# First down projection of a hybrid decoder layer: chunk stores in four pieces on ScalarE's queue in place of one on GpSimd's

## The chip, the core and the metric

The kernel runs on one core of a Trainium2 chip. The time is the device time of one execution in microseconds (us), and a kernel's time is the median over its runs. Five engines work from queues of their own, each in order: TensorE (PE; its weight loads are PEld), VectorE (DVE), ScalarE (ACT), GpSimd (POOL) and SyncE (SP). A DMA is issued by an instruction on one of these queues (here SP, ACT or POOL) and lands later.

## The reference, cut to what matters

One layer, 1024 prompt tokens and 8 x 4 sample tokens, 1024 channels, 2816 hidden units:

```python
x = x + 0.5 * swiglu(rms_norm(x, g_ffn1), w1_ffn1, w3_ffn1, w2_ffn1)   # first FFN
p = rms_norm(x, g_mix) @ w_in        # q, k, v, forget gates, conv inputs
x = x + merge_groups(attention(q, k, v, logf, caches), bg, short_conv(uc), ...)
x = x + 0.5 * swiglu(rms_norm(x, g_ffn2), w1_ffn2, w3_ffn2, w2_ffn2)   # second FFN
```

with `swiglu(x, w1, w3, w2) = (silu(x @ w1) * (x @ w3)) @ w2`. The sample tokens attend to 2048 past positions in pages; `cache_logf` holds a forget value for each past row and head, and is read through the page table. Everything is float32; the kernel makes each product from three matmuls of rounded operands (L104 to L106: high x high, high x low, low x high).

## The kernel before, in words

The 1056 tokens are four chunks of 264, kept with channels on the partitions. The residual `x` of a chunk is 128 x 8 x 264.

**First up projection** (`up`, `blocked`, L277 to L340, and `plain` before it, up to about 92 us). For each block f of 128 hidden units it makes weight sums on DVE, splits them into high and low parts (ACT casts `wh`, L87; DVE subtracts `wl`, L89), and runs products of twelve matmuls each into one of eight PSUM banks (`bank`). DVE takes the products out of the banks and forms `t` = silu(gate) x up, at L326 and L330/L331. POOL stores every `t` to DRAM (`h_d`, L269, L327 and L332). `t` has two buffers: the next-but-one `t` can't be written before the store of the first has landed. Four stores belong to one f for both pairs of chunks, and two to the extra `blocked` call for one pair (f is then called e in `up`).

**First down projection** (`down`, L342). Its work is a list of sections, `DOWN1`: chunk 0 whole, chunks 1 and 2 up to hidden block 12, chunks 1 and 2 from block 12 on, chunk 3 whole. In each, eight output tiles d are computed for each chunk; DVE adds tile d to the residual (L408), ACT squares it (L124) and DVE sums the squares (L125). A tile is final when the chunk's last section has added it. When the chunk's sum of squares is known (`final`, then `done1`, L589), four things follow: the whole chunk is stored to `x_d` by POOL (L590; 1056 KB; the mix stage reads it back later), `rs` is computed (L170/L171), DVE scales all eight tiles **in place** (L190), and the scaled tiles are split into XH and XL (L193/L194), the operands of the mix. The scaling overwrites what the store reads, so it waits until the store has landed.

**past_gates** (L577) fetches the past forget values: 16 times two gathers of 64 KB each into the tile `R` (L468, POOL; `R` has one buffer), and one 128 KB store of `R` to `bs_d` (L587, POOL). It is called in `done1` of chunk 0 inside `tc.issue_after(stored)`.

**What sets the order.** A scheduler puts the instructions of each engine in order when the program is built; source order alone doesn't. `issue_after(ins)` binds what is issued inside it to stand behind `ins`, for the instructions on the engine of `ins`.

```python
t = small("t")                                      # blocked, L329 to L332
nc.vector.tensor_add(t, ps, z["u2"])
nc.vector.tensor_mul(t, t, z["s0"])
nc.gpsimd.dma_start(h_d[2 * p][:, f, :], t)
```

Of the kernel before, what the change touches and what calls it, by code (L numbers as in the profile page):

```python
# [46 lines left out]
DOWN1 = [((0,), 0, NF), ((1, 2), 0, 12), ((1, 2), 12, NF), ((3,), 0, NF)]  # L47
# [15 lines left out]
class Step:  # L63
# [275 lines left out]
            if f % 2 and 0 <= e < n0:  # L339
                self.blocked(w1, w3, e, (1,), ops, h_d)  # L340

    def down(self, w2, h_d, hp, x_of, done, sections, hb, ends=False):  # L342


        nc = self.nc
        xs, accs, sums, sqs, late = {}, {}, {}, {}, []

        def final(c):
            if c in sums:
                nc.tensor.matmul(sums[c], self.ones, sqs[c], start=False, stop=True)  # L350
            else:
                sums[c] = self.bank()
                self.stat(accs[c], sums[c])
            done(c, xs[c], sums[c])

        used, n0 = 0, min(hb, 14)
        before = {}
        for n, (cs, f0, f1) in enumerate(sections):
            end = n == len(sections) - 1
            hs, ins, loads = {}, {}, {}  # L360

            def weights(d):
                ws = []
                for g in range(f0, f1, 8):
                    m = min(8, f1 - g) * P
                    ws += self.weight(w2[d, :, g * P:g * P + m], m)
                loads[d] = self.last
                return ws

            spare = hb - live if n else 0  # L370
            ws = weights(0)
            j = 0
            for c in cs:
                hs[c] = []
                for f in range(f0, f1, 2):
                    u = used % hb
                    p, b = (hp[0], n0) if u < n0 else (hp[1], hb - n0)
                    h = p.tile([P, 2, 2, CH], F32R, tag="h", bufs=b, name="h")
                    used += 1
                    raw = h[:, 1].bitcast(F32)  # L380
                    tie = None
                    if n:
                        tie = before[1 + j * 6 // spare] if j < spare else loads[0]
                    with self.tc.issue_after(tie) if tie else nullcontext():
                        ins[c] = nc.sync.dma_start(raw, h_d[c][:, f:f + 2, :]).ins
                    j += 1
                    self.parts(h[:, 0], h[:, 1], raw)
                    hs[c] += [(h[:, 0, i, :], h[:, 1, i, :]) for i in range(2)]
            live = j
            for d in range(KD):  # L390
                if d:
                    self.after = ins[cs[0]] if d < 2 else None
                    ws = weights(d)
                    self.after = None
                if d == KD - 1:
                    before = loads
                for c in cs:
                    o = self.bank()
                    k = (f1 - f0) // 2
                    self.dot(o, ws[:k], hs[c][:k], stop=False)  # L400
                    if late and d % 4 == 0 and c == cs[-1]:
                        final(late.pop(0))
                    self.dot(o, ws[k:], hs[c][k:], start=False)
                    if d == 0 and f0 == 0:
                        with self.tc.issue_after(ins[c]) if n == 0 else nullcontext():
                            xs[c] = x_of(c)
                    x = xs[c][:, d, :]
                    nc.vector.scalar_tensor_tensor(x, o, 0.5, x, ALU.mult, ALU.add)  # L408
                    if f1 < NF:
                        continue  # L410
                    if ends and end:
                        if d == 0:
                            sums[c] = self.bank()
                        else:
                            nc.tensor.matmul(sums[c], self.ones, sqs[c], start=d == 1, stop=False)
                        sqs[c] = self.small("sq", 4)
                        nc.scalar.activation(sqs[c], x, AF.Square)
                    else:
                        if d == 0:
                            accs[c] = self.tmp.tile([P, CH], F32, tag="acc", bufs=2, name="acc")  # L420
                        self.sq_add(accs[c], d == 0, x)
                    if d == KD - 1:
                        late.append(c)
        for c in late:
            final(c)
# [3 lines left out]
def kernel(ctx: ExitStack, tc: tile.TileContext, io: dict):  # L429
    nc = tc.nc  # L430
    K = Step(tc, io)
# [6 lines left out]
    def pool(es, name, side="right", **kw):  # L438
        return es.enter_context(tc.tile_pool(name=name, bufs=1, side=side, reuse_waits="tile", **kw))
# [17 lines left out]
    def gain(col, k):  # L457
        return prm[:, col + k:col + k + 1]
# [8 lines left out]
    def gather(dst, src, ix):  # L467
        nc.gpsimd.indirect_dma_start(out=dst, out_offset=None, in_=src,  # L468
                                     in_offset=bass.IndirectOffsetOnAxis(ap=ix, axis=0))


    x_d = [dp.tile([P, KD, CH], F32, name=f"x_d{c}") for c in range(NCH)]
    x2_d = [dp.tile([P, KD, CH], F32, name=f"x2_d{c}") for c in range(NCH)]
    h1_d = [dp.tile([P, NF, CH], F32, name=f"h1_d{c}") for c in range(NCH)]
# [94 lines left out]
    with ExitStack() as es:  # L569
        hp = [pool(es, "h1", "left"), pool(es, "h1b", "left")]  # L570
        xp = pool(es, "x2")
        K.tmp = pool(es, "t2")

        def x_in(c):
            x = xp.tile([P, KD, CH], F32, tag="x", bufs=2, name="x")
            nc.sync.dma_start(x, io["xT"][c])
            return x  # L577

        def past_gates():

            for g in range(2):
                for i in range(8):
                    R = K.tmp.tile([P, 2, P], F32, tag="R", bufs=1, name="R")
                    for s in range(2):
                        col = PAGES - 1 - (2 * i + s)
                        gather(R[:, s, :], io["lf"], idl[:, g, col:col + 1])
                    nc.gpsimd.dma_start(bs_d[g][:, 256 * i:256 * i + 256], R.rearrange("p s k -> p (s k)"))  # L587

        def done1(c, x, ps):  # L589
            stored = nc.gpsimd.dma_start(x_d[c], x).ins  # L590
            rs = K.rstd(ps, D)
            cs = slice(c * CH, (c + 1) * CH)
            for k0 in range(0, KD, 4):
                for d in range(k0, k0 + 4):
                    K.scale(x[:, d, :], x[:, d, :], gain(G_MIX, d), rs)
                K.parts(XH[:, k0:k0 + 4, cs], XL[:, k0:k0 + 4, cs], x[:, k0:k0 + 4, :])
            if c == 0:
                with tc.issue_after(stored):
                    past_gates()

        K.nrs = 1
        K.down(io["w2a"], h1_d, hp, x_in, done1, DOWN1, 16, False)
    es_ps.close()

    es_w.close()
# [616 lines left out]
    with ExitStack() as es:  # L1222
        K.tmp = pool(es, "t3")
        xp = pool(es, "x3")
        xa, xs = [None] * NCH, [None] * NCH
# [66 lines left out]
    hp = [pool(ctx, "h2", "left"), pool(ctx, "h2b", "left")]  # L1292
# [118 lines left out]
```

## Time and profile before

| | us |
|---|---|
| median of 3 runs (lowest, highest) | 2117.48 (2117.12, 2118.97) |
| the profiled execution's own time | 2112.15 |
| its span, first to last instruction | 2110.1 |
| PE busy in the span | 2052.3 (97%) |
| DVE, ACT, POOL busy | 1344.5 (64%), 864.9 (41%), 336.2 (16%) |

The profile is of one execution. A timeline row gives the start and the length of an instruction, its engine and line, what it writes and reads, how many like it follow one another, and in brackets how long its engine had been idle and what ended that. Idle time of an engine counts only if the engine that bounds the kernel waits for it. The granted clock is TensorE's, as a share of 2.4 GHz.

### The profile page before, as it was taken

What the parts mean: (1) busy time and instruction counts of PE and PEld (TensorE: products, weight loads), DVE (VectorE), ACT (ScalarE), POOL (GpSimd) and SP (SyncE); (2) the same over time, 40 slices, a digit from 0 to 9 for tenths busy, and PEclk for the clock granted to TensorE, in tenths of its full rate; (3) what the DMA queues carried; (4) which work ended last, traced back from release to release, by engine and by line L of the source; (5) the groups of instructions that cost most, each with busy time, mean ns of one, the idle gap of its engine ahead of it and who ended that gap; (6) DMA issues with size and microseconds to landing.
All of it is one profiled execution on the core that took longest, in us unless ns stands there. A gap on an engine that the chain in (4) does not pass through costs nothing.

```text
span 2110.1 us, 44486 instructions
## 1 busy us (share of the span) xinstructions
PE 2052.3 (97%) x17570; PEld 1969.2 (93%) x17570; DVE 1344.5 (64%) x2586; ACT 864.9 (41%) x1734; POOL 336.2 (16%) x487
## 2 busy tenths in 40 slices
PE   7999999999999889999999989999999999999998
PEld 7999999999999878789997768999999999999997
DVE  8877777777645753222226777886777777775364
ACT  6533333345434432212116664553333343464243
POOL 0011111110233023343433410000101111100000
PEclk9999999999999999999999999999999999999999
DMA  6222222247655679997858525422222222586353
GB/s 217 79 92 93 90 86 87 86 140 267 230 165 171 212 233 349 358 349 236 286 164 194 138 60 177 138 95 81 82 72 83 82 92 87 169 305 200 109 182 126
DMA packets 139617, 341.02 MB, mean 162 GB/s; under 512 B 30000, under 2 KB 46592, under 8 KB 137872
## 3 DMA queue, kind: packets, MB, share of 16 engines
q1 hardware_dynamic: 82704, 218.15, 32.1%
q0 software_dynamic: 28736, 88.50, 12.5%
q10 hardware_dynamic: 27968, 31.54, 4.8%
q8 instruction: 138, 2.26, 0.5%
q14 instruction: 71, 0.58, 0.1%
HBM read 279.75 MB, written 58.33 MB: 160 GB/s over the span
## 4 chain that ended last, share of the span: by engine, by line
PE 55%; DVE 3%; ACT 1%; DMA 1%; issue 1%; POOL 0%; SPq 0%; ACTq 0%; DVEq 0%; POOLq 0%
PE ps L105 12%; PE ps L104 12%; PE ps L106 12%; PE pg L104 4%; PE pg L106 4%; PE pg L105 4%; PE pv L884 1%; PE sc L841 1%; PE O L1157 1%; PE ptp L1143 1%; DVE nm L1129 1%; PE S L1124 1%; PE ps L143 1%; DMA KA<-k_d 1%; DVE Pr L1134 0%
## 5 line engine op out<-in xcount | busy, mean ns | idle before, releaser
L105 PE MATMUL ps<-op,wh 128*128 128x264 f32 x2604 | 741.0, 285 | 1.1 <-DVE op L194 1.0
L106 PE MATMUL ps<-op,wl 128*128 128x264 f32 x2604 | 738.2, 284 | 0.0
L104 PE MATMUL ps<-op,wh 128*128 128x264 f32 x2604 | 737.4, 284 | 0.4 <-ACT s L265 0.4
L87 ACT CAST wh<-wraw 128x512 fp32r<-128x512 f32 x542 | 315.9, 600 | 464.8 <-PE ps L105 297.7
L105 PEld LDWEIGHTS ps<-op,wh 128*128 128x128 f32 x2604 | 489.1, 188 | 2.2 <-DVE op L194 1.9
L104 PEld LDWEIGHTS ps<-op,wh 128*128 128x128 f32 x2604 | 489.5, 188 | 1.2 <-ACT s L265 0.6
L106 PEld LDWEIGHTS ps<-op,wl 128*128 128x128 f32 x2604 | 490.2, 188 | 0.2
L89 DVE TENSOR_TENSOR wl<-wraw,wh 128x512 fp32r<-128x512 f32 x542 | 350.6, 662 | 204.0 <-ACT wh L87 189.9
L106 PE MATMUL ps<-h,wl 128*128 128x264 f32 x1408 | 398.9, 283 | 8.8 <-DVE wl L89 8.8
L104 PE MATMUL ps<-h,wh 128*128 128x264 f32 x1408 | 402.6, 286 | 0.0
L105 PE MATMUL ps<-h,wh 128*128 128x264 f32 x1408 | 401.1, 285 | 0.0
L106 PEld LDWEIGHTS ps<-h,wl 128*128 128x128 f32 x1408 | 265.7, 189 | 9.0 <-DVE wl L89 9.0
L104 PEld LDWEIGHTS ps<-h,wh 128*128 128x128 f32 x1408 | 265.5, 189 | 0.2
L105 PEld LDWEIGHTS ps<-h,wh 128*128 128x128 f32 x1408 | 265.5, 189 | 0.2
L104 PE MATMUL pg<-XH,wh 128*128 128x352 f32 x576 | 190.4, 331 | 0.9 <-DVE z L698 0.9
L106 PE MATMUL pg<-XH,wl 128*128 128x352 f32 x576 | 185.7, 322 | 1.3 <-DVE wl L89 1.1
L105 PE MATMUL pg<-XL,wh 128*128 128x352 f32 x576 | 185.4, 322 | 0.0
L87 ACT CAST wh<-s 128x512 fp32r<-128x512 f32 x176 | 107.8, 616 | 117.3 <-PE ps L105 108.2
L327 POOL DMA_DIRECT2D h_d<-t x79 | 42.8, 542 | 600.4 <-DVE t L326 596.3
L89 DVE TENSOR_TENSOR wl<-s,wh 128x512 fp32r<-128x512 f32 x176 | 120.4, 689 | 25.9 <-ACT wh L87 21.3
L104 PEld LDWEIGHTS pg<-XH,wh 128*128 128x128 f32 x576 | 108.6, 189 | 18.0 <-issue 16.8
L106 PEld LDWEIGHTS pg<-XH,wl 128*128 128x128 f32 x576 | 108.7, 189 | 1.8 <-DVE wl L89 1.8
(273 smaller groups left out, 2576.0 us busy)
## 6 DMA issues: line engine op xcount, KB each, us to landing
wraw<-in_w2a SPq DMA_DIRECT2D x48, 512.0 KB
wraw<-in_w2b SPq DMA_DIRECT2D x48, 512.0 KB
h_d<-t POOLq DMA_DIRECT2D x176, 132.0 KB, 2.0
h<-h_d SPq DMA_DIRECT2D x88, 264.0 KB
kvraw<-in_kc SPq DMA_DIRECT2D x64, 256.0 KB
kvraw<-in_vc SPq DMA_DIRECT2D x64, 256.0 KB
wraw<-in_w1a SPq DMA_DIRECT2D x28, 512.0 KB
wraw<-in_w3a SPq DMA_DIRECT2D x28, 512.0 KB
```

The source lines that it names most:

```text
L87: nc.scalar.copy(wh, x)
L89: nc.vector.tensor_sub(wl, x, wh)
L104: nc.tensor.matmul(ps, w[0], x[0], start=start, stop=False)
L105: nc.tensor.matmul(ps, w[0], x[1], start=False, stop=False)
L106: nc.tensor.matmul(ps, w[1], x[0], start=False, stop=stop)
L143: nc.tensor.matmul(ps, self.ones, sq, start=n == 0, stop=n == len(xs) - 1)
L327: nc.gpsimd.dma_start(h_d[2 * p + 1][:, f, :], t)
L841: nc.tensor.matmul(ps[quarter(hp)], QZ[:, g, hp, 32 * b4:32 * b4 + 32], raw[:, :, hp * P:hp * P + P], start=b4 == 0, stop=b4 == 3)
L884: nc.tensor.matmul(pv[quarter(hp), cs], PT[:, 4 * j + s, quarter(hp)], raw[:, s, hp * P:hp * P + P], start=j == 0 and s == 0, stop=False)
L1124: nc.tensor.matmul(S[:, k0:k1], QA[:, qs], KA[:, k0:k1], start=True, stop=False)
L1129: nc.vector.tensor_reduce(nm, S[:, :nk], AX.X, ALU.max, negate=True)
L1143: nc.tensor.transpose(pt_[:, j * P:(j + 1) * P], Pr[:, (j0 + j) * P:(j0 + j + 1) * P], ident)
```

## The change

`down` gets a function `part`, which it calls after every second output tile of a chunk's last section (d = 1, 3, 5, 7). The first down projection passes `store`, which stores two finished tiles (128 x 528, 264 KB) from ACT's queue. `done1` no longer stores. `past_gates` stays inside `issue_after`, which now names the last piece of chunk 0, an instruction on ACT.

```diff
-    def down(self, w2, h_d, hp, x_of, done, sections, hb, ends=False):
+    def down(self, w2, h_d, hp, x_of, done, sections, hb, ends=False, part=None):
...
                     if f1 < NF:
                         continue
+                    if part and d % 2:
+                        part(c, xs[c], d - 1)
...
+        stored = {}
+
+        def store(c, x, d):
+            stored[c] = nc.scalar.dma_start(x_d[c][:, d:d + 2, :], x[:, d:d + 2, :]).ins
+
         def done1(c, x, ps):
-            stored = nc.gpsimd.dma_start(x_d[c], x).ins
             rs = K.rstd(ps, D)
...
             if c == 0:
-                with tc.issue_after(stored):
+                with tc.issue_after(stored[0]):
                     past_gates()
...
-        K.down(io["w2a"], h1_d, hp, x_in, done1, DOWN1, 16, False)
+        K.down(io["w2a"], h1_d, hp, x_in, done1, DOWN1, 16, False, store)
```

In the changed file lines behind L410 lie two lower, and those behind L590 six lower: the gathers are L470, the store to `bs_d` is L589, the pieces are L594.

The order of instructions on PE is the same. On POOL it is not. This is POOL's order of the changed kernel against that of before in the first up projection, from the last store of `plain` (L269) over the stores of f = 6 (L327, L332) to the first of f = 7. `h1_d` is the DRAM copy of the hidden units; `R` and `bs_d` belong to `past_gates`.

```order
 L269 DMA h1_d1_84<-t_1115 128x264
+L470 DMA R_7390<-in_lf,idl_73 128x128 x2
+L589 DMA bs_d0_119<-R_7390 128x256
+L470 DMA R_7394<-in_lf,idl_73 128x128 x2
+L589 DMA bs_d0_119<-R_7394 128x256
+L470 DMA R_7398<-in_lf,idl_73 128x128 x2
 L327 DMA h1_d1_84<-t_1399 128x264
 L327 DMA h1_d3_86<-t_1417 128x264
+L589 DMA bs_d0_119<-R_7398 128x256
 L332 DMA h1_d0_83<-t_1433 128x264
+L470 DMA R_7402<-in_lf,idl_73 128x128 x2
 L332 DMA h1_d2_85<-t_1450 128x264
```

Gathers now stand ahead of and between the stores of `t`. The pattern goes on over f = 7, 8 and 9; this is its end, up to the stores of the extra call with e = 0.

```order
 L332 DMA h1_d2_85<-t_2248 128x264
+L589 DMA bs_d1_120<-R_7446 128x256
+L470 DMA R_7450<-in_lf,idl_73 128x128 x2
+L589 DMA bs_d1_120<-R_7450 128x256
 L327 DMA h1_d3_86<-t_2385 128x264
 L332 DMA h1_d2_85<-t_2401 128x264
```

All 32 gathers and 16 stores of `R` stand ahead of the store of `t_2385`. In the down projection the same 48 instructions are gone from POOL, and with them the whole-chunk stores; the last rows of that piece of the difference:

```order
-L468 DMA R_7447<-in_lf,idl_73 128x128 x2
-L587 DMA bs_d1_120<-R_7447 128x256
-L590 DMA x_d1_76<-x_7342 128x2112
-L590 DMA x_d2_77<-x_7469 128x2112
-L701 MEMSET zt_10018 128x72
-L590 DMA x_d3_78<-x_9006 128x2112
```

Before, the stores of chunks 1 and 2 stood behind the whole of `past_gates`. On ACT the last pieces of chunks 1 and 2 now stand in front of the squares of the same tiles (`sq`), several casts ahead of `rs` and XH of chunk 1 (ACT of the changed kernel):

```order
L594 DMA x_d1_76<-x_7346 128x528
L124 ACTIVATE sq_8814<-x_7346 128x264
...
L594 DMA x_d2_77<-x_7472 128x528
L124 ACTIVATE sq_8850<-x_7472 128x264
...
L170 ACTIVATE rs_8968<-ps_8961,eps_68 128x264
...
L193 CAST XH_6374<-x_7346 128x4x264
```

## Rows read from the trace of the kernel before

**Rows 1.** The page's busy time, share of span and instructions of each engine.

```profile
PE 2052.3 (97%) x17570; PEld 1969.2 (93%) x17570; DVE 1344.5 (64%) x2586; ACT 864.9 (41%) x1734; POOL 336.2 (16%) x487
```

**Rows 2.** PE's waits, 470 to 840 us: total us, times, longest.

```profile
PE ps L106 <- DVE wl L89: 8.8, 1, 8.8
PE ps L135 <- ACT ah L133: 2.3, 1, 2.3
...
PE pg L104 <- DVE z L698: 0.9, 1, 0.9
```

**Rows 3.** Timeline of PE around its longest wait: start, us, instruction, idle before.

```profile
683.51 0.28 PE L105 MATMUL ps<-h,wh 128*128 128x264 f32 x1
692.61 0.59 PE L106 MATMUL ps<-h,wl 128*128 128x264 f32 x1 [8.81 <-DVE wl L89]
...
697.38 0.28 PE L106 MATMUL ps<-h,wl 128*128 128x264 f32 x1
```

**Rows 4.** Timeline of DVE, 660 to 700 us.

```profile
674.80 1.80 DVE L171 RECIPROCAL rs<-rs 128x264 f32<-128x264 f32 x1
676.51 0.63 DVE L89 TENSOR_TENSOR wl<-wraw,wh 128x512 fp32r<-128x512 f32 x1
687.71 2.92 DVE L190 SCALAR_TENSOR_TENSOR x<-x,prm,rs 128x264 f32<-128x264 f32 x7 [10.57 <-DMA x_d<-x]
```

**Rows 5.** Timeline of POOL, 540 to 690 us.

```profile
543.98 1.02 POOL L468 DMA_INDIRECT R<-in_lf,idl  x1 [0.56 <-DMA wraw<-in_w2a]
...
590.06 0.97 POOL L468 DMA_INDIRECT R<-in_lf,idl  x1 [1.85 <-DMA bs_d<-R]
...
603.91 0.97 POOL L468 DMA_INDIRECT R<-in_lf,idl  x1 [1.94 <-DMA bs_d<-R]
...
652.05 0.96 POOL L468 DMA_INDIRECT R<-in_lf,idl  x1 [3.50 <-DMA bs_d<-R]
...
658.53 0.97 POOL L468 DMA_INDIRECT R<-in_lf,idl  x1 [1.86 <-DMA bs_d<-R]
...
678.27 0.97 POOL L468 DMA_INDIRECT R<-in_lf,idl  x1 [3.58 <-DMA bs_d<-R]
...
682.71 0.59 POOL L587 DMA_DIRECT2D bs_d<-R  x1 [2.22 <-DMA R<-in_lf,idl]
683.29 1.10 POOL L590 DMA_DIRECT2D x_d<-x  x2
```

**Rows 6.** Timeline of DVE at chunk 3's end.

```profile
745.55 1.67 DVE L764 COPY selh<-cst 8x128 f32<-8x128 f32 x1
...
753.92 2.92 DVE L190 SCALAR_TENSOR_TENSOR x<-x,prm,rs 128x264 f32<-128x264 f32 x7 [3.87 <-DMA x_d<-x]
```

**Rows 7.** The DMA issues: count, KB each, median us to landing.

```profile
h_d<-t POOLq DMA_DIRECT2D x176, 132.0 KB, 2.0
...
x_d<-x POOLq DMA_DIRECT2D x4, 1056.0 KB, 6.1
```

**Rows 8.** Windows: us, busy (count) of PE, PEld, DVE, ACT, POOL, clock, DMA share, GB/s.

```profile
92.00:183.00 91.00, 91.00 (x752) 91.00 (x751) 72.80 (x144) 35.33 (x73) 8.95 (x17) 1.00 0.27 86
544.00:683.00 139.00, 139.00 (x1149) 139.00 (x1149) 74.89 (x138) 55.37 (x103) 43.75 (x48) 1.00 0.56 183
683.00:698.00 15.00, 6.19 (x34) 5.98 (x33) 9.44 (x17) 4.11 (x6) 1.39 (x3) 0.66 0.65 235
...
590.00:604.00 14.00, 14.00 (x118) 14.00 (x117) 3.80 (x7) 1.71 (x4) 5.09 (x7) 1.00 0.20 55
```

**Rows 9.** Timeline of POOL, 85 to 185 us.

```profile
182.71 0.54 POOL L327 DMA_DIRECT2D h_d<-t  x1 [7.68 <-DVE t L326]
```

**Rows 10.** Timeline of DVE, 88 to 113 us.

```profile
90.52 1.25 DVE L230 TENSOR_TENSOR d<-x,d 128x1056 f32<-128x1056 f32 x1
...
112.69 0.43 DVE L330 TENSOR_TENSOR t<-ps,u 128x264 f32<-128x264 f32 x1 [0.58 <-DMA h_d<-t]
```

**Rows 11.** Line L468's gathers of `R`: duration ns min/median/max, first and last start.

```profile
L468 POOL DMA_INDIRECT R<-in_lf,idl x32: 941/972/1565, 544.0 to 679.5; - x32
```

## The prediction, as it stood before the changed kernel was run

> **What bounds the kernel now.** I read the page first, for which engine bounds the span: PE is busy in 97% of it [rows 1]. A change can only give back what PE waits, or make it wait anew, so the next view is PE's waits around the first down projection. Three are worth naming: 8.8 us for a `wl` of DVE, 2.3 us for `ah` of ACT, and 0.9 us for DVE's `z` [rows 2]. PE's timeline then shows the large one as a hole: the last matmul before it starts at 683.51, the next at 692.61 [rows 3].
>
> DVE's timeline says why that `wl` was late. DVE works in order. It made its last `wl` before the hole at 676.51 (0.63 long), then sat idle for 10.57 us, until 687.71, in front of the scaling of chunk 1, and what ended the idle time was the landing of an `x_d` store [rows 4]. POOL's timeline says why the store was late: `past_gates` fills POOL's queue from 543.98 until the last `bs_d` store at 682.71, and the two `x_d` stores stand right behind it, at 683.29 [rows 5]. The tiles of chunk 1 had long been final, since `rs`, which is made from all of them, starts at 674.80 [rows 4]. So the hole is a queueing delay on POOL, and the change takes the store off that queue.
>
> **What goes.** *The hole.* 692.61 − 683.51 is 9.1 us, less the one step of 0.12 that would be there anyway (91.0 us for 752 matmuls, [rows 8]): 9.0 us. After it PE runs slowly: the 21 steps from 692.61 to 697.38 take 4.77 us [rows 3] where 21 × 0.121 are 2.5. That is the granted clock, 0.66 as the mean of this stretch and 1.00 in the others [rows 8]: PE had stood still for 9 us, and was at the lower of its two levels (1.2 of 2.4 GHz) for a time. So 2.2 us more, and **11.2 us** in all.
>
> Does all of it go? The last piece of chunk 1 is issued before the squares, so before 674.80. A piece is 264 KB; the median store of 132 KB lands after 2.0 us, one of 1056 KB after 6.1 [rows 7]. At the very latest it has landed at 674.8 + 6.1 = 680.9, and it is likely down by 677.1, when DVE comes to the scaling. From the start of the scaling to the matmul behind the hole were 4.9 us (687.71 to 692.61). So PE's `wl` comes at 682.0, in time, or at worst at 685.8, 2.2 us late. I take 682.0: all 11.2 us.
>
> *Chunk 3.* DVE waits 3.87 us for its store too, but PE feels only the 0.9 us of `z` [rows 2, 6]. Against that, DVE's copy `selh` (1.67 us, [rows 6]) now stands ahead of the last sum of squares, on which `ah` rests, and PE waits for `ah`. Gain up to 0.9, loss up to 1.7: I set the two at nothing, and keep both ends for the range.
>
> *The cost of the pieces.* Sixteen more issues on ACT. ACT's own issue has no row here; POOL's of 0.54 us [rows 9] bounds it: 16 × 0.54 = 8.6 us, spread over a stage in which ACT is busy 55 of 139 us [rows 8]. Each piece waits for the tile that the square behind it waits for as well, so ACT is held no longer than before: nothing. The bytes are the same, and 16 landings overlap. The four issues taken from POOL are worth nothing to PE. SP has one `h` load one place earlier: nothing.
>
> **What is moved, and this decides.** The diff leaves `past_gates` in its place, but `issue_after` bound POOL's gathers to a POOL instruction, and the new one is ACT's. Nothing holds the gathers on POOL now, and the order shows where they went: 32 gathers and 16 stores of `R` now stand in the first up projection, among POOL's stores of `t`. There the cover is thin: DVE is busy 72.8 of 91 us [rows 8], and it already waits for a store's landing before it may write `t`, as at 112.69 [rows 10]. If POOL's queue is late, the stores of `t` are late, DVE stops at L330 with both buffers of `t` in use, and behind it in DVE's queue stand the `wl` that PE needs and the evictions that free PSUM.
>
> How late? The first gather waits for what last used the space of `R`; the latest of this I found in the rows is a DVE subtraction that ends at 90.52 + 1.25 = 91.8 [rows 10], so it starts at 92.0. `R` has one buffer, so pairs run one after another: two gathers, their landing, the store, its landing. A pair took 13.85 / 2 = 6.93 us between 590.06 and 603.91, where the DMA engines were busy 0.20, and (678.27 − 543.98) / 15 = 8.95 us on average from the first to the last, where it was 0.56; the quickest took 6.48 (652.05 to 658.53) [rows 5, 8]. In the up projection the share is 0.27 [rows 8], which on the line between the two means is 7.3 us; the gathers add some 0.1 of their own, which gives 7.9. I take **T = 7.5 us**, between them. The stores of `t` that stand inside a pair issue in 0.54 us while it waits for a landing, at no cost.
>
> The last pair starts at 92.0 + 15 × 7.5 = 204.5. From its start to the end of its store's issue are 682.71 + 0.59 − 678.27 = 5.0 us [rows 5]. So the store of `t` behind it, which before was issued at 182.71 [rows 9], goes out at 209.5, **26.8 us late**. PE doesn't feel it all. With eight banks it may run seven products ahead of a stopped DVE: 7 × 12 × 0.121 = 10.2 us, if its `wl` are made. 26.8 − 10.2 = 16.6, and 2.2 us for the lower clock after such a stop, as above: **18.8 us lost**, as holes between about 150 and 210 us.
>
> **The sum.** 18.8 − 11.2 = +7.6 us. The profiled execution took 2112.15 us, span 2110.1, and would take 2119.8; it lies 5.3 us under the median of the runs, 2117.5, so the same step from the median gives **2125.1 us**. As a formula: loss = 15 T − 93.7, so the kernels are equal at T = 6.99 us. At the quickest pair, 6.48, the loss is 3.5 and the time 2109.8. At 8.95 the loss is 40.6 and the time 2146.8. If slack covers everything it is 2106.3.
>
> **Two rules weighed.** The rows show that 10.57 us of waiting ended with a store that had been queued behind other work [rows 4, 5]. The Trainium skill (Trainium Kernel Development and Optimization, Key Constraints) says that DMAs from SP, ACT and POOL share the same 16 DMA engines, and that issuing from several engines saves only the sequencer's issue time. By that alone the change would save four issues of POOL's, some 2 us, none of them PE's, and the time would come out with the loss and without the gain. The rows speak against taking it so: what stands ahead in an in-order queue costs more than an issue.
>
> A gather's issue took 941 to 1565 ns [rows 11], a spread that its size does not explain. The Trainium skill (SBUF — State Buffer, Who interferes with whom) says that descriptors of POOL's DMAs are starved while DVE holds the port that the two share. By it the gathers would slow where DVE is busiest, which is the up projection. No row here shows a gather there; POOL's store of `t` takes its 0.54 us beside a DVE that is 80% busy [rows 8, 9], which speaks against much of it.
>
> **The rivals.**
> - *Faster: the queue keeps up.* If a pair takes less than 6.71 us, or DVE and PSUM absorb more than I reckon, the hole goes and little comes back: 2106 to 2113. For it: pairs of 6.48 did occur. Against it: only at the quick end, and DVE is at 80%.
> - *A draw.* T from 6.71 to 7.27, as the quiet mean of 6.93 would have it: 2113 to 2121.
> - *Gain missing.* The hole at 683 stays, because the pieces land late or ACT's queue holds them, as the first rule would have it; then the loss stands alone: 2117.5 + 18.8 = 2136. Against it: 674.8 + 6.1 us lies before the hole.
> - *Slow gathers.* Pairs at the loaded mean of 8.95, by traffic or, as the second rule has it, by starved descriptors: 32 issues at 1565 in place of 972 ns are 19 us more, which is 1.2 us a pair, and T = 8.7 gives 2143. So 2139 to 2147.
>
> **How the numbers follow.** A difference of 0.2%, 4.2 us, is about what a measurement can tell from none. Forecast (T from 7.27 to about 8.4): 0.40. Queue keeps up: 0.22. Draw: 0.20. Gain missing: 0.06. Slow gathers: 0.12. So faster 0.22, same 0.20, slower 0.58. The likeliest case's own range is 2122 to 2138. The range for 8 in 10 reaches down to the quickest pair and up past the missing gain: 2109 to 2139; outside it are full cover and the slow gathers.
>
> **What would show it.** Right: gathers from 92 us on, pairs of about 7.5 us, the last to 205; DVE's waits for `h_d` stores at L330 grown from the 0.58 of one row to some 10 us; PE waiting 15 to 19 us there, partly at the lower clock; no hole at 683, and scaling of chunk 1 from about 677. Wrong: gathers elsewhere, or no new wait of PE before 210 us (the queue is covered, and the kernel faster), or a hole at 683 in spite of pieces landed before 680 (then the store was not its cause).

## The result, and the profile after

The changed kernel takes 2129.95 us (median of 4 runs, 2129.0 to 2133.55) where the kernel before takes 2117.3 (4 runs, 2114.6 to 2118.97): a ratio of 1.0055, 95% interval 1.0035 to 1.0074. It is slower by 12.7 us; forecast were 7.6 us and a range of 2109 to 2139. Its profiled execution took 2130.66 us (span 2128.8), 0.7 over its median, where that of before lay 5.2 under its own: of the 18.5 us between the two profiles some 6 are the spread of the runs.

The first place to look is the up projection. These are PE's waits there, 90 to 300 us of the changed kernel (us in total, times, longest), where before there were none:

```profile
PE ps L104 <- DVE t L330: 16.9, 4, 7.8
```

DVE's waits in the same stretch, first row:

```profile
DVE t L330 <- DMA h_d<-t: 43.2, 13, 10.6
```

DVE waits for stores of `t` to land before it may write `t`, and PE waits for DVE. POOL's timeline says why the stores are late (start, us, instruction, idle before it):

```profile
93.28 5.35 POOL L470 DMA_INDIRECT R<-in_lf,idl  x1 [1.20 <-DVE d L230]
98.93 1.50 POOL L470 DMA_INDIRECT R<-in_lf,idl  x1 [0.30 <-issue]
102.52 0.58 POOL L589 DMA_DIRECT2D bs_d<-R  x1 [2.09 <-DMA R<-in_lf,idl]
106.69 0.97 POOL L470 DMA_INDIRECT R<-in_lf,idl  x1 [3.59 <-DMA bs_d<-R]
...
199.59 0.59 POOL L327 DMA_DIRECT2D h_d<-t  x1
...
211.57 0.99 POOL L470 DMA_INDIRECT R<-in_lf,idl  x1 [1.96 <-DMA bs_d<-R]
...
216.90 0.59 POOL L589 DMA_DIRECT2D bs_d<-R  x1 [2.70 <-issue]
217.48 0.58 POOL L327 DMA_DIRECT2D h_d<-t  x1
```

The pairs begin at 93.28, the sixteenth at 211.57, so one takes 118.29 / 15 = 7.89 us on average. They are not alike: the first, from 93.28 to 106.69, took 13.41 us, and the fourteen after it (211.57 − 106.69) / 14 = 7.49. The store of `t` behind them goes out at 217.48 where it was 182.71 [rows 9]: 34.8 us late. Rows without idle time, as 217.48, are stores that had been ready and stood in the queue.

The clock took its share too. Windows of the changed kernel (us, busy and count of PE, PEld, DVE, ACT, POOL, granted clock, DMA share, GB/s):

```profile
130.00:160.00 30.00, 25.58 (x189) 25.36 (x188) 15.45 (x33) 7.59 (x19) 13.22 (x16) 0.89 0.27 89
160.00:190.00 30.00, 22.25 (x163) 22.03 (x162) 14.26 (x30) 6.67 (x16) 11.67 (x16) 0.83 0.28 89
190.00:220.00 30.00, 26.00 (x194) 25.82 (x193) 19.61 (x42) 9.78 (x23) 14.02 (x18) 0.89 0.36 116
```

PE did 546 matmuls in these 90 us, at 0.121 us each the work of 66. Of the 24 us lost some 16 are waits of PE (three long stops, of 4.4, 7.8 and 4.0 us), and the rest goes with the lower granted clock, which each of the three windows shows; in the kernel before it was 1.00 [rows 8].

The gain is there as well. DVE's timeline at chunk 1:

```profile
701.51 1.80 DVE L171 RECIPROCAL rs<-rs 128x264 f32<-128x264 f32 x1
703.23 0.63 DVE L89 TENSOR_TENSOR wl<-wraw,wh 128x512 fp32r<-128x512 f32 x1
703.77 2.90 DVE L190 SCALAR_TENSOR_TENSOR x<-x,prm,rs 128x264 f32<-128x264 f32 x7
```

The scaling follows the `wl` without the 10.57 us of idle time it had [rows 4], and the hole of PE is gone from the page's group of these matmuls, whose idle time (the last column) of 8.8 us was the hole. Before, then after:

```profile
L106 PE MATMUL ps<-h,wl 128*128 128x264 f32 x1408 | 398.9, 283 | 8.8 <-DVE wl L89 8.8
```

```profile
L106 PE MATMUL ps<-h,wl 128*128 128x264 f32 x1408 | 397.7, 282 | 0.0
```

`rs` shows how the account stands on the way: 674.80 before [rows 4], 701.51 now, 26.7 us late (0.65 of it from the start, where the last store of `plain` is at 91.55 in place of 90.90). At the end of the down projection PE comes to `ah` of chunk 3 at 761.58 where it was 746.13. Before, then after:

```profile
746.13 0.39 PE L135 MATMUL ps<-ah,ones_r 128*128 128x264 f32 x1 [2.33 <-ACT ah L133]
```

```profile
761.58 0.59 PE L135 MATMUL ps<-ah,ones_r 128*128 128x264 f32 x1 [2.72 <-ACT ah L133]
```

15.45 us late: 11.3 have come back. The span ends 18.7 us late. About 2 us of what was lost after `ah` stand at chunk 3 itself. PE has short gaps there that the profile puts down to "issue" (2.1 us in sum), but before it waited there too (0.8 us for `al` and 0.9 for `z`); what differs more is the granted clock of the first 14 us, 0.88 before and 0.77 now:

```profile
746.00:760.00 14.00, 12.13 (x64) 9.55 (x65) 8.92 (x15) 4.07 (x7) 11.08 (x12) 0.88 1.04 334
```

```profile
761.50:775.50 14.00, 13.01 (x61) 9.97 (x61) 7.26 (x12) 2.03 (x4) 10.41 (x11) 0.77 1.02 353
```

### The profile page after: what moved, and what is told of

Its sections match the earlier page's. It is cut to its first block, busy times and chain, and to the rows that moved or that the text cites. A ratio compares the mean times of both kernels' runs of the same rounds, so it can differ in the third digit from the quotient of the medians.

```text
span 2128.8 us, 44477 instructions
## 1 busy us (share of the span) xinstructions
PE 2062.0 (97%) x17570; PEld 1977.1 (93%) x17570; DVE 1338.4 (63%) x2586; ACT 857.4 (40%) x1734; POOL 336.4 (16%) x483
## 4 chain that ended last, share of the span: by engine, by line
PE 55%; DVE 4%; ACT 2%; issue 1%; DMA 1%; POOL 0%; SPq 0%; ACTq 0%; DVEq 0%; POOLq 0%
PE ps L105 12%; PE ps L104 12%; PE ps L106 12%; PE pg L104 4%; PE pg L106 4%; PE pg L105 4%; PE pv L890 1%; PE sc L847 1%; PE O L1163 1%; PE ptp L1149 1%; PE S L1130 1%; PE S L1131 1%; PE ps L143 1%; ACT Pr L1138 1%; DMA KA<-k_d 1%
## 5 line engine op out<-in xcount | busy, mean ns | idle before, releaser
L104 PE MATMUL ps<-op,wh 128*128 128x264 f32 x2604 | 742.0, 286 | 17.3 <-DVE t L330 16.9
L327 POOL DMA_DIRECT2D h_d<-t x79 | 43.0, 544 | 524.5 <-DVE t L326 504.8
L105 PEld LDWEIGHTS pg<-XL,wh 128*128 128x128 f32 x576 | 108.8, 189 | 1.7 <-issue 1.7
```

The costliest lines, as they stand in the source:

```text
L104: nc.tensor.matmul(ps, w[0], x[0], start=start, stop=False)
L105: nc.tensor.matmul(ps, w[0], x[1], start=False, stop=False)
L327: nc.gpsimd.dma_start(h_d[2 * p + 1][:, f, :], t)
```

## The experiments

The theory: the whole loss is the gathers among the stores of `t`, the whole gain is that the `x_d` stores no longer stand behind `past_gates`; both come from the place in POOL's queue, and nothing from the pieces or from ACT. Ratios are to the kernel before, run on the same chip, with their 95% intervals. Not all runs shared a chip, and the same program differed by up to 0.4% in its ratio from one chip to the next (e8_sp and e10_sp below), so smaller differences between chips rest on the traces; `held` is the load of the page table in POOL's queue, issued at about 479 us, when all stores of `t` are out.

**Gain alone (e1_tied).**

```diff
-    nc.gpsimd.dma_start(pt, ...)
+    held = nc.gpsimd.dma_start(pt, ...).ins
...
-                with tc.issue_after(stored[0]):
+                with tc.issue_after(held):
                     past_gates()
```

> The changed kernel, but past_gates tied to a POOL instruction again (the load of the page table, issued at 479 us in the kernel before), so that its gathers stand behind the stores of t. The orders on PE, ACT and DVE are those of the changed kernel. Theory (the loss is the gathers among the stores of t, the gain is the x_d stores off the queue of past_gates, and the two add up): no wait of PE for t, no hole at 683 us, 2117.3 - 11 = 2106 us (2103 to 2109), 24 us under the changed kernel. Rival (the pieces and ACT's queue bring the loss): at or above 2117 us, with the waits of PE where they are in the changed kernel.

Measured: 2107.41 us, 0.9941 (0.9922 to 0.9960). PE's waits between 90 and 700 us are one row:

```profile
PE ps L136 <- DVE al L134: 0.3, 1, 0.3
```

Only POOL's order differs from the changed kernel, so the loss is in that order, and the rival falls: pieces on ACT cost nothing that shows.

**Loss and gain without the pieces (e2_untied).**

```diff
-                with tc.issue_after(stored):
-                    past_gates()
+                past_gates()
```

> The kernel before, whole stores on POOL, with the tie of past_gates taken away and nothing else. Theory: the gathers go to the up projection by themselves, and the x_d stores are then alone on POOL, so loss and gain both appear: 2127 to 2133 us, as the changed kernel, with four waits of PE for t, 17 us in sum, and no hole at 683; that is, the pieces and ACT's queue bring nothing. Rival (the gain needs the pieces or another queue): the hole at 683 stays, and the time is 2138 to 2143 us.

Measured: 2136.25 us, 1.0072 (1.0051 to 1.0093), an interval that overlaps that of the changed kernel; the median lies 3 us above the expected range, while the ratio times 2117.3, 2132.5, lies in it. PE's waits, 90 to 740 us:

```profile
PE ps L104 <- DVE t L330: 18.0, 4, 8.4
PE ps L106 <- DVE wl L89: 2.6, 1, 2.6
```

The large hole goes without pieces and without another queue. The expectation of none was a little off: 2.6 us stay. That is not the wait for the store; the scaling starts with no idle time before it:

```profile
704.95 1.80 DVE L171 RECIPROCAL rs<-rs 128x264 f32<-128x264 f32 x1
706.66 0.63 DVE L89 TENSOR_TENSOR wl<-wraw,wh 128x512 fp32r<-128x512 f32 x1
707.21 2.91 DVE L190 SCALAR_TENSOR_TENSOR x<-x,prm,rs 128x264 f32<-128x264 f32 x7
```

Here `rs` comes later against PE, and the scaling itself then delays the next `wl`. ACT's rows say why `rs` is late: two pairs of casts `wh` stand ahead of it and wait for weights. Before, then e2_untied:

```profile
671.27 1.14 ACT L87 CAST wh<-wraw 128x512 fp32r<-128x512 f32 x2 [0.36 <-DMA wraw<-in_w2a]
672.59 1.14 ACT L87 CAST wh<-wraw 128x512 fp32r<-128x512 f32 x2 [0.18 <-DMA wraw<-in_w2a]
```

```profile
698.98 1.14 ACT L87 CAST wh<-wraw 128x512 fp32r<-128x512 f32 x2 [2.94 <-DMA wraw<-in_w2a]
702.74 1.14 ACT L87 CAST wh<-wraw 128x512 fp32r<-128x512 f32 x2 [2.62 <-DMA wraw<-in_w2a]
```

The whole stores of chunks 1 and 2, now issued at 690.86 and 695.50, run beside these loads, at a DMA share of 0.99:

```profile
695.00:700.00 5.00, 5.00 (x44) 5.00 (x43) 1.63 (x4) 1.98 (x4) 0.53 (x1) 1.00 0.99 400
```

e3_early (below), whose stores are whole and on POOL too, has the same waits of ACT (3.23 and 2.64 us) and a wait of PE of 2.87; the kernels with the stores on ACT or SP have at most 0.2 there. That the whole stores hold up the weights is likely, but no run varied it alone. So the pieces or the other queue may be worth these 2.6 us, against the theory's nothing.

**Loss alone (e7_extra).** The kernel before, with a second set of gathers and stores of `R`, untied; `extra` is a copy of `past_gates` that stores to `bs2_d`:

```diff
             if c == 0:
+                extra()
                 with tc.issue_after(stored):
                     past_gates()
```

> The kernel before, and beside its own past_gates a second, untied one that writes to a DRAM buffer nobody reads; the order puts it where the changed kernel has its gathers. It is the suspected loss alone, with the hole at 683 us left in. Theory: 2117.3 + 24 to 26 = 2141 to 2144 us. Rival (gathers between the stores of t cost little, and the changed kernel lost its time elsewhere): under 2125 us.

Measured: 2147.31 us, 1.0118 (1.0095 to 1.0142), that is 25 us by the ratio and 29 by the medians; the median lies 3 us above the expected range. PE's waits, 90 to 740 us:

```profile
PE ps L104 <- DVE t L330: 17.6, 4, 7.9
PE ps L106 <- DVE wl L89: 11.3, 1, 11.3
```

The changed kernel's four waits and the hole of before, here 2.5 us longer, side by side. Loss alone is +1.18%, gain alone −0.59%; their sum of +0.59% agrees, within the intervals, with the +0.55% of the change and the +0.72% of e2_untied.

**More buffers for `t` (e5_four_t).**

```diff
-                t = small("t")
+                t = small("t", 4)
```

> The changed kernel with four buffers for t in place of two; gathers stay in the up projection. Theory (DVE stops because both buffers of t wait for a store that POOL has not issued): two more buffers let DVE run on for two more stores, some 10 us of the 20 us that four take, so the waits of PE shrink from 17 to about 5 to 8 us, and the time is 2117 to 2122 us. Rival (the gathers slow the stage by their traffic or by holding DVE): buffers do not matter, 2128 to 2132 us.

Measured: 2129.08 us, 1.0044 (1.0030 to 1.0058): a miss, since the time hardly moved. PE's waits, 90 to 300 us:

```profile
PE ps L104 <- issue: 13.7, 1, 13.7
PE ps L104 <- DVE t L330: 3.5, 1, 3.5
PE ps L104 <- DVE u L323: 2.3, 1, 2.3
```

They came later (from 178 us) and in sum are no smaller. The time is what the rival said, and by itself it would carry the rival. The stores speak for the theory: the first store of f = 9 is 40.1 us late against e1_tied, not 30.5 (table below), and PE is hardly later than in the changed kernel, so the buffers absorbed some 9 us more, and the queue took as much back: a pair took (218.86 − 93.75) / 15 = 8.34 us. Why pairs took longer is open, and the gathers' own cost may have a part in it, so this run doesn't decide; the next one says more.

**A shorter walk (e6_half_R).**

```diff
-                    R = K.tmp.tile([P, 2, P], F32, tag="R", bufs=1, name="R")
                     for s in range(2):
+                        R = K.tmp.tile([P, P], F32, tag="R", bufs=2, name="R")
...
```

> The changed kernel, gathers still among the stores of t, but R as two half tiles with a store of 64 KB each, in the same space, so that one gather runs while the other half is stored. It shortens the walk of the queue alone. A half takes about 1 (issue) + 2.1 (landing) + 0.6 (issue of the store) + 1.9 (its landing) = 5.6 us, two in flight, so a pair takes some 5.6 us in place of 7.9. Theory (lateness of the queue sets the loss): 93.3 + 15 x 5.6 + 5 = 182 us, where the store behind was issued at 182.7 in the kernel before: PE's waits for t under 4 us, 0.994 to 0.998 of the kernel before. Rival (the loss is set by the number of gathers, by their traffic or by DVE being held): 1.003 or more, with PE's waits for t above 12 us.

Measured: 2118.64 us, 1.0020 (1.0011 to 1.0030), PE's waits 90 to 740 us:

```profile
PE ps L104 <- DVE t L330: 11.2, 3, 4.6
```

Between the two expectations. A pair took (191.15 − 92.73) / 15 = 6.56 us, not 5.6 (11.22 the first, 6.23 the others on average), so the queue was still late; the same bytes and the same 32 gathers cost less when the walk is shorter: PE comes to `ah` 16.3 us late, not 24.7. With 32 stores of `R` in place of 16 and their traffic no smaller, that speaks against the rival. Three kernels with the gathers in the up projection can now be set against e1_tied, which has none there (first store of f = 9 at 169.07 us, PE's matmul on `ah` at 736.84):

| | first store of f = 9 | late by | PE at `ah` | late by | absorbed |
|---|---|---|---|---|---|
| e6_half_R | 192.13 | 23.1 | 753.14 | 16.3 | 6.8 |
| changed | 199.59 | 30.5 | 761.58 | 24.7 | 5.8 |
| e5_four_t | 209.14 | 40.1 | 761.85 | 25.0 | 15.1 |

With two buffers some 6 to 7 us of lateness are absorbed and every further us is PE's; two more buffers absorb 9 more.

**What stands ahead of a store (e3_early).** The kernel before with `issue_after(held)`, whole stores on POOL.

> The kernel before with whole stores on POOL, and past_gates tied to the load of the page table, some 64 us earlier than its tie of before. The order then has the store of chunk 0 behind 12 of the 16 pairs, and those of chunks 1 and 2 behind all. Theory (what counts is what stands ahead of a store on its in-order queue): the hole at 683 is gone, but a new one stands in front of the scaling of chunk 0. In e1_tied a pair took 10.25 us in this stage; 481 + 12 x 7 to 10 = 565 to 604 us is when the store is issued, where before it was 543, and DVE is ready for the scaling at 555: a hole of PE of 10 to 45 us there, and 1.00 to 1.016 of the kernel before. Rival (the hole at 683 came from the gathers' traffic or from the store's own landing, not from its place): no new hole, and the old one stays, 1.00.

Measured: 2137.37 us, 1.0105 (1.0087 to 1.0122). PE's waits 90 to 740 us, the scaling of chunk 0, and POOL at that store:

```profile
PE ps L106 <- DVE wl L89: 34.5, 3, 31.4
```

```profile
594.50 2.92 DVE L190 SCALAR_TENSOR_TENSOR x<-x,prm,rs 128x264 f32<-128x264 f32 x7 [39.74 <-DMA x_d<-x]
```

```profile
589.11 0.95 POOL L468 DMA_INDIRECT R<-in_lf,idl  x1 [0.30 <-issue]
590.06 0.58 POOL L590 DMA_DIRECT2D x_d<-x  x1
```

The hole moved to the chunk whose store now stands behind the gathers: the tie alone, without the stores off POOL, costs 22 us. That settles the cause of the hole; the 2.87 us that stay at chunk 1 have another (above).

**Pieces or whole, ACT or SP (e4_whole, e8_sp, e9_act, e10_sp).** All have `issue_after(held)`. e4_whole stores each chunk whole in `done1` on ACT; e8_sp and e10_sp issue the pieces on SP; e9_act is e1_tied again.

```diff
-            stored[c] = nc.scalar.dma_start(...)
+            stored[c] = nc.sync.dma_start(...)
```

> As e1_tied, but each chunk is stored whole by one DMA on ACT's queue in done1, not in four pieces; past_gates is tied to the load of the page table. It tells what the pieces are worth once nothing stands ahead of the stores. Theory (only the queue ahead mattered): ACT issues the store of chunk 1 before rs, at about 670 us, it lands some 6 us later, no hole for chunk 1; chunk 3 keeps its wait of about 1 us: within 3 us of e1_tied, that is 0.994 to 0.996 of the kernel before. Rival (small early pieces matter): a hole of 3 us or more for chunk 1, 0.997 or more.

> As e1_tied, with the pieces issued on SP's queue in place of ACT's. The order has weight loads and loads of h behind each piece, and a piece waits for its tile. Theory: SP runs far enough ahead for the loads that little is late; the time is that of e1_tied or up to 8 us more, 0.994 to 0.998. If SP's lead is short, its weight loads stop behind pieces that wait for tiles, PE shows new waits between 500 and 740 us, and the time is above 1.00.

Measured: e4_whole 2103.90 us, 0.9950 (0.9933 to 0.9966); e8_sp 2099.68 us, 0.9927 (0.9912 to 0.9941). In e4_whole the scaling of chunk 1 waits 0.56 us for its whole store, and PE doesn't feel it:

```profile
676.15 3.32 DVE L190 SCALAR_TENSOR_TENSOR x<-x,prm,rs 128x264 f32<-128x264 f32 x8 [0.56 <-DMA x_d<-x]
```

So pieces are worth nothing measurable against one whole store on ACT. e8_sp came out under its expected range and looked better than e1_tied, and its chunk 3 had no short gaps. Whether that is the queue was tried on one chip:

> The kernel of e1_tied again, beside e8_sp's on one chip, since their ratios (0.9941 and 0.9927) came from two chips. Theory: with pieces on ACT, the order on ACT puts the second half of chunk 3's XH behind the second z, which waits for PE, and PE then waits some 2 us for that half (747 to 752 us in e1_tied's trace): 0.994 to 0.995 of the kernel before.

> The kernel of e8_sp again, beside e9_act. Theory: the same gain from the tie, and no wait of PE for XH at chunk 3: 2 to 5 us under e9_act, 0.992 to 0.9935 of the kernel before. Rival (the two differ by chip alone): within 1 us of e9_act.

Measured: e9_act 2108.28 us, 0.9971 (0.9955 to 0.9987); e10_sp 2107.04, 0.9968 (0.9956 to 0.9980). Both lie above what was expected of them, 1.2 us apart, which is about what the rival said; and e10_sp has gaps at chunk 3 that e8_sp lacked, the longest of them:

```profile
751.22 0.45 PE L105 MATMUL pg<-XL,wh 128*128 128x352 f32 x1 [1.71 <-issue]
```

The theory falls: the order of the second XH is not their cause, and what is stays open. The five runs of the tied versions gave 0.9927 to 0.9971: each beats both kernels, by 7 to 16 us against before, and no one of them is shown to be the best.

## Why the prediction was right, and where it was off

- **The mechanism** was as forecast: the lost tie, the gathers ahead of the stores of `t`, DVE stopped at L330 and PE behind it; the hole at 683 gone, the scaling of chunk 1 right behind its `wl`. e1_tied and e7_extra show each side alone.
- **The gain** of 11.2 us for the hole: 11.3 came back between `rs` of chunk 1 and `ah` of chunk 3; 11.1 us by the medians of e1_tied, 7.0 by those of e9_act, the same kernel on another chip. With the stores freed but still whole on POOL, 2.6 (e2_untied) and 2.9 us (e3_early) of PE's wait stayed, with late weights and not the store ahead of them.
- **The lateness of the queue** is the term that was mis-sized: 26.8 us forecast, 34.8 measured. Fifteen pairs took 118.3 us, not 112.5 (5.8), the first began at 93.28, not 92.0 (1.3), and the last took 5.9 to the end of its store's issue, not 5.0 (0.9). The 5.8 are the first pair alone: it took 13.41 us, and the other fourteen 7.49 on average, just what the forecast took for all. A first pair that is longer was to be seen in the kernel before, where it took 10.54 us (543.98 to 554.52) and the others 8.84, but there its first gather took only 1.02 us [rows 5], not 5.35.
- **What PE absorbs** came out near by two errors that cancel. I took 10.2 us for the banks and gave 2.2 back for one spell of the lower clock, 8.0 net. Measured: 34.8 less the 26.1 by which `rs` was late (26.7 less 0.65) is 8.7 net; the table under e6_half_R, which goes by an earlier store and a later matmul, gives 5.8. But PE's four waits sum to 16.9, so stops alone absorbed far more, and the lower clock and slow spells cost the other 9 us: a queue that is late in several places stops PE several times, and each long stop had its own spell. That the net came out near is luck.
- **Chunk 3** was set at nothing within −0.9 and +1.7; it cost about 2 us, just outside, in a stretch with the granted clock at 0.77 in place of 0.88. The copy `selh` that I feared was not the cause: it took 0.40 us.
- **The two rules.** The Trainium skill (Trainium Kernel Development and Optimization, Key Constraints) holds that another issuing engine saves only issue time. With nothing ahead in the queue that is what the runs show: ACT and SP, pieces and whole come out alike. What the move changed here was the order on an engine, which that sentence doesn't speak of. The descriptors that the Trainium skill says are starved beside DVE (SBUF — State Buffer, Who interferes with whom) don't show: the median gather took 992 ns in the up projection, 972 in the down projection [rows 11]. The forecast read that section too widely: it has a DVE instruction stall a DMA of POOL's in the two-port modes, and says that `tensor_tensor`, which is all of DVE's work in this stretch, did not.

```profile
L470 POOL DMA_INDIRECT R<-in_lf,idl x32: 941/992/5346, 93.3 to 212.9; - x32
```

## What to carry to other kernels

When an instruction is moved to another engine, look for what was ordered by it on the old one: a tie that holds only on its own engine is lost, the diff hardly hints at it, and the order of the built program is where it shows. A queue that is late costs what the stage behind it can't absorb, so off-path work on an in-order queue belongs where nobody waits for that queue. Here the change alone lost 12.7 us and the new tie alone (e3_early) lost 22; the two together gained 7 to 11 (e9_act, e1_tied).

## What the runs showed that was not expected

- **A small copy beside POOL.** `selh` took 1.67 us before [rows 6], next to POOL's memsets; in the changed kernel, where they run earlier, 0.40 us. POOL of before, then DVE of the changed kernel:

```profile
745.50 1.19 POOL L623 MEMSET QZ<- 128x1280 f32 x1
746.60 0.55 POOL L628 MEMSET VS<- 128x512 f32 x1
```

```profile
760.33 0.40 DVE L770 COPY selh<-cst 8x128 f32<-8x128 f32 x1
```

  Before, the copy ended at 747.22, just behind the memsets at 747.15. The Trainium skill (SBUF — State Buffer, Who interferes with whom) says that a copy of DVE and an instruction of POOL can hold one port against each other for a whole instruction; these rows agree with it, though no run here varied it alone.
- **A pair's time goes with the traffic.** Without the first pair, the mean was 7.49 us at a DMA share of 0.30, and 9.86 in e1_tied at 0.67. The line through the kernel before, 6.93 at 0.20 and 8.84 (again without the first pair) at 0.56 [rows 5, 8], gives 7.5 and 9.4. No run varied the traffic alone. The shares of the changed kernel and of e1_tied:

```profile
92.00:218.00 126.00, 109.08 (x830) 108.29 (x829) 75.22 (x151) 35.29 (x79) 56.79 (x66) 0.91 0.30 97
```

```profile
480.00:640.00 160.00, 159.67 (x1316) 159.46 (x1316) 93.63 (x169) 70.08 (x129) 46.91 (x48) 1.00 0.67 226
```

- **The first pair.** Its first gather took 5.35 us in the changed kernel and 4.44 in e1_tied, but 1.02 before [rows 5]. The first pair was the longest in the changed kernel and in e1_tied (13.41 and 15.67 us), and of the 8.0 us by which the forecast of the queue was short it made 5.8. No run tells why.
